# Expert layers of a two-block kernel: the second table as the streamed operand of its products

## The chip, the core and the metric

The kernel runs on one core of a Trainium2 chip. The metric is the device time of one execution in microseconds (us). Engines are named as the profile names them: PE is TensorE (matrix products; PEld is its loading of the stationary operand, the weights), DVE is VectorE, ACT is ScalarE, POOL is GpSimd, and SP is SyncE, whose queue issues the DMAs here.

## What is computed

The reference is a chain of two blocks of two layers each, over 256 tokens of 1024 features, all in fp32. The change lies in the two expert layers (`peer_ffn`, one in each layer of the first block). Each has 16384 experts; an expert is a row of a first table `u_tab` and a row of a second table `v_tab`:

```python
def block(args):
    hx, idx, g = args                      # 128 tokens, their chosen experts, gates
    u = u_tab[idx]
    act = jax.nn.gelu(jnp.einsum('thkd,td->thk', u, hx).astype(jnp.float32))
    return jnp.einsum('thk,thkd->td', g * act, v_tab[idx])
...
mod = (cond @ w_ada[i] + b_ada[i])[:, None, :]
sh1, sc1, g1, sh2, sc2, g2 = jnp.split(mod, 6, axis=-1)
...
x = x + g2 * peer_ffn(h, peer_w_q[i], peer_keys[i], peer_u[i], peer_v[i])
```

The second thing of interest is the modulation, `mod`: a product of one vector with a table of 1024 by 6144 for each layer. The part of it for layer 1 that is left is computed during the expert layer of layer 0.

## The kernel before, in words

**Data.** Activations lie features by tokens: a tile has 128 features on its partitions and 256 tokens along its columns. Every product is made of three products of a rounded format (fp32r): each operand is split into a high part and the rest, and high x high, high x rest and rest x high are added up in PSUM. `mm3` (lines 414 to 419) issues the three: L416 weight high and activation high, L417 weight high and activation rest, L418 weight rest and activation high. In the trace they read `psmm<-xh,whi`, `psmm<-xl,whi` and `psmm<-xh,wlo`: the output, then the streamed operand, then the stationary one.

**Weights.** A `Stream` (lines 255 to 296) reads a table in blocks of 128 partitions by 1024 columns (512 KB). A block lands in one of four `raw` buffers; ACT casts it to `whi` (L283), DVE subtracts to get `wlo` (L285); there are three buffers of each. SP's queue is strictly in order: a DMA that waits for its buffer holds all DMAs behind it.

**The expert layer** (`peer`, from line 1151). It does not gather rows. It multiplies the tokens with all of the first table (128 chunks of 128 experts), applies gelu and the gates (zero for experts that a token didn't choose), and keeps the result in `A`, 128 experts by 128 chunks by 256 tokens. The change is in what follows, the sum over the second table. For each chunk `c` of 128 experts (`chunk`, L1253) one block of V is read and split; every second chunk also splits two chunks of `A` into `xh` (ACT, L464) and `xl` (DVE, L465), which are called `wh` and `wl` in the code. `product` (L1259) then makes, for each of the eight groups `o` of 128 features, the three products with a 128x128 piece of V as the stationary operand and 256 tokens as the streamed one: 24 products of 256 columns for a chunk. The sums, features by tokens, collect in four PSUM banks over all 128 chunks. I call this stretch the V stage, V0 in layer 0 and V1 in layer 1.

**The modulation in V0.** `ada_sums` (L704) reads 48 blocks of 512 KB through the same `raw` buffers; for each DVE issues one product-and-add with a running row (L712 and L714, written to `oh`), and after every eight PE adds the row up over partitions (L718). In the code a step is issued after every second chunk from chunk 9 on.

**The end of the stage.** The last three chunks are held back (`last`) and run feature group by feature group. While a pair of groups is in work, the evacuation of the pair before runs: `residual` (L743) adds the sum to the residual (L753, DVE), makes the next projection's leading operand (`lead.tile`: L314 on ACT, L315 on DVE) and squares for the norm (L487, ACT). `lead.products` are 96 products of the next layer's first projection that need no norm; the rest of that projection waits for the norm (L503, L504, L551, L552).

**Order.** A scheduler sets the order on each engine's queue from the code's dependences and its own costs; engines then run their queues in order.

Of the kernel before, what the change touches and what calls it, by code (L numbers as in the profile page):

```python
# [114 lines left out]
WO = 1, 2  # L115
SQB = 2
NST = 4
PL = 1, 3
ADDED, ADDED_LN = 6, 4

# [134 lines left out]
class Stream:  # L255
# [1 line left out]

    def __init__(s, ker, name, lo_pool=None, hi_dve=None, store=()):  # L260
        s.ker, s.name, s.ap = ker, name, ker.d[name]
        s.lo_pool, s.hi_dve, s.store = lo_pool, hi_dve, store
        s.b = 0
        s.tiles = []

    def prefetch(s, pin=False):

        k, b = s.ker, s.b
        if b == s.ap.shape[0]:
            return  # L270
        s.b += 1
        nc = k.nc
        keep = k.pin if pin else lambda ins: ins
        raw = k.raw_block(s.ap[b])
        if b < len(s.store):
            hi, lo = s.store[b]
        else:
            hi = k.splp.tile([128, WBLK], F32R, name="whi", tag="whi")
            lo = k.splp.tile([128, WBLK], F32R, name="wlo", tag="wlo")
        if s.hi_dve and s.hi_dve(b):  # L280
            keep(nc.vector.tensor_copy(hi, raw))
        else:
            keep(nc.scalar.copy(hi, raw))  # L283
        eng = nc.gpsimd if s.lo_pool and s.lo_pool(b) else nc.vector
        keep(eng.tensor_tensor(lo, raw, hi.bitcast(F32), op=OP.subtract))  # L285
        s.tiles += [(hi[:, j * 128:(j + 1) * 128], lo[:, j * 128:(j + 1) * 128]) for j in range(8)]

    def __iter__(s):
        return s
# [53 lines left out]
class Ker:  # L343
# [357 lines left out]
                                                   op0=OP.add, op1=OP.subtract)  # L701
        return hi, lo

    def ada_sums(s, layer, r, acc):  # L704
# [446 lines left out]
    def peer(s, layer, x):  # L1151
# [3 lines left out]
        with s.tc.tile_pool(name="peer", bufs=1) as P:  # L1155
# [91 lines left out]
                        applied = S  # L1247

            wh, wl = s.acts()
            acc = [s.mm().rearrange("p (a b) -> p a b", a=2) for _ in range(4)]  # L1250
            vt = s.stream(f"V{layer}")

            def chunk(c):  # L1253
                if c % 2 == 0:
                    sl = slice(c % 8, c % 8 + 2)
                    s.split_into(wh[:, sl, :], wl[:, sl, :], A[:, c:c + 2, :])
                return [next(vt) for _ in range(KD)], (wh[:, c % 8, :], wl[:, c % 8, :])

            def product(c, o, v, w):  # L1259
                s.mm3(acc[o // 2][:, o % 2, :], v[o], w, c == 0 and o % 2 == 0, c == NK - 1, skip_group_check=True)  # L1260

            extra = iter(())
            if layer == 0:
                extra = chain(*(s.ada_sums(1, r, oh.rearrange("p a b c d -> p (a b c d)").bitcast(F32)[:, 0:WBLK])
                                for r in range(3)))
            NL = 3
            for c in range(NK - NL):
                v, w = chunk(c)
                for o in range(KD):
                    product(c, o, v, w)  # L1270
# [15 lines left out]
            for j in range(KD // 2):  # L1286
                for o in (2 * j, 2 * j + 1):
                    for c, v, w in last:
                        product(c, o, v, w)
                for f in after:  # L1290
                    f()
                after = [ev(o, acc[j][:, o % 2, :]) for o in (2 * j, 2 * j + 1)]
            for f in after:
                f()
            lead.products()
# [529 lines left out]
```

## Time and profile before

| | |
|---|---|
| median of three timed runs | 3094.58 us (3094.17 to 3098.24) |
| the profiled execution | 3085.98 us |
| its span, first to last instruction | 3084.2 us |
| PE busy | 2924.4 us, 95% |
| DVE busy | 2242.0 us, 73% |
| ACT busy | 1489.4 us, 48% |
| POOL busy | 434.6 us, 14% |
| V0, first to last product of V | 785.2 to 1171.0 us |
| V1, last product of V | 2196.0 us |

PE's busy time is of modelled ends: a product of 256 columns is listed with some 0.28 us, while the next one starts about 0.12 us after it. What a product takes of the stage is therefore read from the distance of two starts, not from its listed length. The same holds, less strongly, for DVE: its instructions overlap by a few hundredths of a us.

### The profile page before, as it was taken

How to read it: one execution, taken by the hardware profiler on the slowest of the kernel's cores; microseconds unless marked ns; L12 is line 12 of the kernel's file. 1: busy time of each engine (PE TensorE's matmuls, PEld its weight loads, DVE VectorE, ACT ScalarE, POOL GpSimd, SP SyncE). 2: the span in 40 equal slices, each digit the busy share in tenths (PEclk: the TensorE clock that was granted, in tenths of full speed). 3: DMA queues.
4: the chain of work that ended last, by engine and by line, in shares of the span. 5: the costliest groups of instructions: out<-in, count | busy, mean ns of one | idle time of the engine just before them, and what ended most of it. 6: DMA issues, size and time to landing. Idle time of an engine off the chain costs nothing. (4 is left out here: it accounts for less than half of the span.)

```text
span 3084.2 us, 58197 instructions
## 1 busy us (share of the span) xinstructions
PE 2924.4 (95%) x23408; PEld 2824.4 (92%) x23408; DVE 2242.0 (73%) x4113; ACT 1489.4 (48%) x2576; POOL 434.6 (14%) x260
## 2 busy tenths in 40 slices
PE   7999989999999998698999999999999989998898
PEld 7988989999999997698999999999988889977898
DVE  7897996777567658899777765555663588665885
ACT  3335534444444445554444444444654666555663
POOL 2232330000000003523300000000123020111201
PEclk9999999999999998899999999999999999998999
DMA  6664445444677863354544456655435246543464
GB/s 251 205 189 155 154 140 165 144 145 151 198 260 259 263 218 122 115 168 156 159 143 144 146 159 183 184 184 182 156 100 75 89 145 184 181 123 81 143 185 131
DMA packets 139999, 503.66 MB, mean 163 GB/s; under 512 B 15800, under 2 KB 18504, under 8 KB 139344
## 3 DMA queue, kind: packets, MB, share of 16 engines
q1 hardware_dynamic: 139728, 499.93, 52.8%
q8 instruction: 184, 3.01, 0.4%
q14 instruction: 87, 0.71, 0.1%
HBM read 496.72 MB, written 1.05 MB: 161 GB/s over the span
## 5 line engine op out<-in xcount | busy, mean ns | idle before, releaser
L416 PE MATMUL psmm<-xh,whi 128*128 128x256 f32 x5488 | 1568.4, 288 | 43.2 <-ACT xh L464 18.3
L418 PE MATMUL psmm<-xh,wlo 128*128 128x256 f32 x5488 | 1558.8, 286 | 33.3 <-DVE wlo L285 20.9
L417 PE MATMUL psmm<-xl,whi 128*128 128x256 f32 x5488 | 1564.0, 286 | 3.9 <-DVE xl L465 1.9
L283 ACT CAST whi<-raw 128x1024 fp32r<-128x1024 f32 x819 | 857.5, 1048 | 1094.3 <-PE psmm L417 781.4
L285 DVE TENSOR_TENSOR wlo<-raw,whi 128x1024 fp32r<-128x1024 f32 x740 | 936.6, 1268 | 446.1 <-ACT whi L283 434.0
L416 PEld LDWEIGHTS psmm<-xh,whi 128*128 128x128 f32 x5488 | 1059.9, 194 | 56.0 <-ACT xh L464 19.9
L418 PEld LDWEIGHTS psmm<-xh,wlo 128*128 128x128 f32 x5488 | 1060.3, 194 | 37.9 <-DVE wlo L285 24.1
L417 PEld LDWEIGHTS psmm<-xl,whi 128*128 128x128 f32 x5488 | 1063.1, 194 | 8.1 <-DVE xl L555 3.3
L285 POOL TENSOR_TENSOR wlo<-raw,whi 128x1024 fp32r<-128x1024 f32 x90 | 249.6, 2778 | 460.9 <-ACT whi L283 416.4
L285 POOL TENSOR_TENSOR Ar<-raw,Ar 128x1024 fp32r<-128x1024 f32 x4 | 9.6, 2408 | 1361.1 <-ACT Ar L283 1361.1
L1190 DVE TENSOR_TENSOR oh<-io,sel 128x512 f16<-128x512 f16 x128 | 54.4, 425 | 105.2 <-PE psac L1202 52.7
L416 PE MATMUL psst<-xh,whi 128*128 128x256 f32 x400 | 119.9, 301 | 0.0
L417 PE MATMUL psst<-xl,whi 128*128 128x256 f32 x400 | 118.4, 297 | 0.3 <-DVE xl L646 0.3
L418 PE MATMUL psst<-xh,wlo 128*128 128x256 f32 x400 | 117.9, 295 | 0.7 <-DVE wlo L285 0.7
L1202 PEld LDWEIGHTS <-oh 128*128 128x128 f16 x1024 | 103.8, 118 | 6.9
L416 PE MATMUL psmm<-yh,whi 128*128 128x256 f32 x352 | 98.0, 279 | 0.0
L418 PE MATMUL psmm<-yh,wlo 128*128 128x256 f32 x352 | 97.6, 278 | 0.0
L417 PE MATMUL psmm<-yl,whi 128*128 128x256 f32 x352 | 97.2, 276 | 0.0
L714 DVE SCALAR_TENSOR_TENSOR oh<-raw,cond,oh 128x1024 f32<-128x1024 f32 x42 | 53.9, 1284 | 56.8 <-DMA raw<-in_ada 56.6
L465 DVE TENSOR_TENSOR xl<-A,xh 128x512 fp32r<-128x512 f32 x128 | 87.1, 684 | 0.0
L417 PEld LDWEIGHTS psst<-xl,whi 128*128 128x128 f32 x400 | 79.0, 197 | 7.3 <-issue 5.6
L418 PEld LDWEIGHTS psst<-xh,wlo 128*128 128x128 f32 x400 | 79.0, 198 | 5.0 <-issue 3.5
(574 smaller groups left out, 4031.8 us busy)
## 6 DMA issues: line engine op xcount, KB each, us to landing
raw<-in_U SPq DMA_DIRECT2D x256, 512.0 KB, 3.6
raw<-in_V SPq DMA_DIRECT2D x256, 512.0 KB, 4.2
raw<-in_up SPq DMA_DIRECT2D x88, 512.0 KB, 4.0
raw<-in_ada SPq DMA_DIRECT2D x80, 512.0 KB, 4.4
raw<-in_down SPq DMA_DIRECT2D x44, 512.0 KB, 3.7
raw<-in_ev_in SPq DMA_DIRECT2D x42, 512.0 KB, 3.6
raw<-in_hg_in SPq DMA_DIRECT2D x40, 512.0 KB, 3.9
raw<-in_peer_q SPq DMA_DIRECT2D x32, 512.0 KB, 3.6
```

What stands on the lines that cost most here:

```text
L283: keep(nc.scalar.copy(hi, raw))
L285: keep(eng.tensor_tensor(lo, raw, hi.bitcast(F32), op=OP.subtract))
L416: first = t.matmul(ps, w[0], x[0], start=start, stop=False, **kw)
L417: t.matmul(ps, w[0], x[1], start=False, stop=False, **kw)
L418: t.matmul(ps, w[1], x[0], start=False, stop=stop, **kw)
L465: s.nc.vector.tensor_tensor(lo, src, hi.bitcast(F32), op=OP.subtract)
L714: nc.vector.scalar_tensor_tensor(acc, raw, s.cond[:, k:k + 1], acc, op0=OP.mult, op1=OP.add)
L1190: nc.vector.tensor_tensor(o1, io4, k1, op=OP.is_equal)
L1202: ins = nc.tensor.matmul(pv[:, t, :], oh[:, g % 2, 0, :, t], oh[:, g % 2, 1 + e, :, t], start=e == 0, stop=e == 1)
```

## The change

Three things change.

1. The roles of the operands in the V stage are swapped. `Stream` gets a width, so that V's block is handed on whole. The stationary operand is now a piece of the activations (128 experts by 128 tokens, two token tiles `tt`), the streamed one is half of V's block (512 features, two halves). A chunk has 2 x 2 x 3 = 12 products of 512 columns. Four PSUM banks hold one sum each, of 128 tokens by 512 features.
2. The sums now lie tokens by features. At the end of the stage they are copied to SBUF (`tok`, two copies by ACT and two by DVE, in two `raw` buffers) and transposed back on PE, sixteen transposes of 128x128 in four PSUM tiles; `residual` reads those.
3. The modulation's blocks in V0 no longer share the `raw` buffers. They land in four pieces of `A` that hold the first sixteen chunks, which are used up by then. A step is issued after every second chunk from chunk 17 on.

```diff
-        s.tiles += [(hi[:, j * 128:(j + 1) * 128], lo[:, j * 128:(j + 1) * 128]) for j in range(8)]
+        s.tiles += [(hi[:, j:j + s.width], lo[:, j:j + s.width]) for j in range(0, WBLK, s.width)]
...
-                raw = s.raw_block(s.d[f"ada{layer}"][((r - 1 + layer) * KD + k) * 2 + e])
+                ap = s.d[f"ada{layer}"][((r - 1 + layer) * KD + k) * 2 + e]
+                if room:
+                    raw = room[k % len(room)]
+                    nc.sync.dma_start(raw, ap)
+                else:
+                    raw = s.raw_block(ap)
...
-            acc = [s.mm().rearrange("p (a b) -> p a b", a=2) for _ in range(4)]
-            vt = s.stream(f"V{layer}")
+            acc = [[s.mm() for _ in range(2)] for _ in range(2)]
+            vt = s.stream(f"V{layer}", width=WBLK)
...
-            def product(c, o, v, w):
-                s.mm3(acc[o // 2][:, o % 2, :], v[o], w, c == 0 and o % 2 == 0, c == NK - 1, skip_group_check=True)
+            def product(c, half, tt, v, w):
+                ts, fs = slice(tt * 128, (tt + 1) * 128), slice(half * 512, (half + 1) * 512)
+                for i, (a, b) in enumerate(((0, 0), (0, 1), (1, 0))):
+                    nc.tensor.matmul(acc[half][tt], w[a][:, ts], v[b][:, fs], start=c == 0 and i == 0,
+                                     stop=c == NK - 1 and i == 2)
...
+                room = [Af[:, n * WBLK:(n + 1) * WBLK] for n in range(RAW_A)]
...
-                if c % 2 and c > 8:
+                if c % 2 and c >= 4 * RAW_A:
                     next(extra, None)
...
+            def features(half, tok):
+                for j in range(2):
+                    pt = s.ac().rearrange("p (a b) -> p a b", a=2)
+                    for e in range(2):
+                        for tt in range(2):
+                            nc.tensor.transpose(pt[:, e, tt * 128:(tt + 1) * 128],
+                                                tok[:, tt, (2 * j + e) * 128:(2 * j + e + 1) * 128], s.ident)
+                    yield [ev(4 * half + 2 * j + e, pt[:, e, :]) for e in range(2)]
...
+                    (nc.vector.tensor_copy if tt else nc.scalar.copy)(tok[:, tt, :], acc[half][tt])
```

The scheduler's order changes with it. Three places matter for the prediction.

**PE in the V stage.** Before, two feature groups of one chunk (`psmm_9022` is a bank, `xh` and `xl` the activations' parts, `whi` and `wlo` V's):

```order
L418 MATMUL psmm_9022<-xh_9017,wlo_13085 128x256
L416 MATMUL psmm_9022<-xh_9017,whi_13092 128x256
L417 MATMUL psmm_9022<-xl_9018,whi_13092 128x256
L418 MATMUL psmm_9022<-xh_9017,wlo_13093 128x256
L416 MATMUL psmm_9022<-xh_9017,whi_13098 128x256
```

Now, one whole chunk:

```order
L1271 MATMUL psmm_9019<-whi_11544,xh_9017 128x512
L1271 MATMUL psmm_9020<-whi_11544,xh_9017 128x512
L1271 MATMUL psmm_9021<-whi_11544,xh_9017 128x512
L1271 MATMUL psmm_9022<-whi_11544,xh_9017 128x512
L1271 MATMUL psmm_9019<-wlo_11545,xh_9017 128x512
L1271 MATMUL psmm_9019<-whi_11544,xl_9018 128x512
L1271 MATMUL psmm_9020<-wlo_11545,xh_9017 128x512
L1271 MATMUL psmm_9020<-whi_11544,xl_9018 128x512
L1271 MATMUL psmm_9021<-wlo_11545,xh_9017 128x512
L1271 MATMUL psmm_9021<-whi_11544,xl_9018 128x512
L1271 MATMUL psmm_9022<-wlo_11545,xh_9017 128x512
L1271 MATMUL psmm_9022<-whi_11544,xl_9018 128x512
```

Half as many products of twice the width; the four that need only the high part come first, in four banks.

**DVE and SP in V0.** Before, on DVE (`oh` is the modulation's running row, `raw_9399` and `raw_9464` its blocks):

```order
L285 TENSOR_TENSOR wlo_9306<-raw_9303,whi_9305 128x1024
L714 SCALAR_TENSOR_TENSOR oh_3390<-raw_9399,cond_90,oh_3390 128x1024
L285 TENSOR_TENSOR wlo_9342<-raw_9339,whi_9341 128x1024
L465 TENSOR_TENSOR xl_9018<-A_2917,xh_9017 128x512
L285 TENSOR_TENSOR wlo_9372<-raw_9369,whi_9371 128x1024
L714 SCALAR_TENSOR_TENSOR oh_3390<-raw_9464,cond_90,oh_3390 128x1024
```

Now, on DVE:

```order
L286 TENSOR_TENSOR wlo_9350<-raw_9347,whi_9349 128x1024
L719 TENSOR_SCALAR oh_3390<-A_2917,cond_90 128x1024
L721 SCALAR_TENSOR_TENSOR oh_3390<-A_2917,cond_90,oh_3390 128x1024
L466 TENSOR_TENSOR xl_9018<-A_2917,xh_9017 128x512
L721 SCALAR_TENSOR_TENSOR oh_3390<-A_2917,cond_90,oh_3390 128x1024
L286 TENSOR_TENSOR wlo_9373<-raw_9370,whi_9372 128x1024
L721 SCALAR_TENSOR_TENSOR oh_3390<-A_2917,cond_90,oh_3390 128x1024
L286 TENSOR_TENSOR wlo_9391<-raw_9388,whi_9390 128x1024
```

and on SP's queue in the same stretch, before and now:

```order
L395 DMA raw_9464<-in_ada1 128x1024
L395 DMA raw_9469<-in_V0 128x1024
L395 DMA raw_9499<-in_V0 128x1024
L395 DMA raw_9529<-in_ada1 128x1024
L395 DMA raw_9534<-in_V0 128x1024
```

```order
L396 DMA raw_9468<-in_V0 128x1024
L715 DMA A_2917<-in_ada1 128x1024
L396 DMA raw_9490<-in_V0 128x1024
L715 DMA A_2917<-in_ada1 128x1024
L396 DMA raw_9508<-in_V0 128x1024
L715 DMA A_2917<-in_ada1 128x1024
```

The 48 modulation steps stood one to two chunks from chunk 7 to chunk 106; they now stand about one to a chunk, on DVE from chunk 3 to chunk 54 of V0.

**PE at the end of V0.** Before, the last product of V is followed by those of the next layer (`Ar` holds the leading operand and its weights):

```order
L417 MATMUL psmm_9022<-xl_9018,whi_13098 128x256
L418 MATMUL psmm_9022<-xh_9017,wlo_13099 128x256
L416 MATMUL psac_13247<-Ar_13103 128x258
L416 MATMUL psac_13248<-Ar_13103 128x258
L416 MATMUL psmm_13249<-Ar_13103 128x258
```

Now the transposes (`cst` holds the identity) stand between:

```order
L1271 MATMUL psmm_9022<-whi_11550,xl_9018 128x512
L1307 MATMUL psac_11622<-cst_80,tok_11580 128x128
L1307 MATMUL psac_11637<-cst_80,tok_11580 128x128
L1307 MATMUL psac_11622<-cst_80,tok_11580 128x128 x3
L1307 MATMUL psac_11637<-cst_80,tok_11580 128x128 x3
L1307 MATMUL psac_11654<-cst_80,tok_11601 128x128 x4
L417 MATMUL psmm_11691<-Ar_11555 128x258
```

All twelve products of the last chunk run before the first transpose, and the first addition to the residual comes behind both of DVE's copies.

## Rows read from the trace of the kernel before

**Rows 1.** The page: busy time by engine; PE's clock in 40 slices.

```profile
PE 2924.4 (95%) x23408; PEld 2824.4 (92%) x23408; DVE 2242.0 (73%) x4113; ACT 1489.4 (48%) x2576; POOL 434.6 (14%) x260
...
PEclk9999999999999998899999999999999999998999
```

**Rows 2.** Groups by form, V1 from 1850 to 2150: count | busy, mean ns | idle.

```profile
L418 PE MATMUL psmm<-xh,wlo 128*128 128x256 f32 x834 | 236.0, 283 | 0.0
L416 PE MATMUL psmm<-xh,whi 128*128 128x256 f32 x834 | 236.0, 283 | 0.0
L417 PE MATMUL psmm<-xl,whi 128*128 128x256 f32 x834 | 236.0, 283 | 0.0
...
L285 DVE TENSOR_TENSOR wlo<-raw,whi 128x1024 fp32r<-128x1024 f32 x105 | 128.6, 1225 | 142.5 <-ACT whi L283 142.5
L283 ACT CAST whi<-raw 128x1024 fp32r<-128x1024 f32 x105 | 109.9, 1047 | 165.4 <-PE psmm L417 165.4
```

**Rows 3.** Busy time in stretches: start, V0, its end, half clock, V1.

```profile
core 0: us, PE busy (x) PEld busy (x) DVE busy (x) ACT busy (x) POOL busy (x), PEclk, DMA share, GB/s
10.00:30.00 20.00, 17.70 (x127) 15.60 (x125) 18.73 (x26) 4.93 (x9) 5.14 (x2) 1.00 1.03 409
768.00:870.00 102.00, 94.37 (x768) 91.97 (x767) 59.36 (x65) 43.72 (x56) 0.00 (x0) 1.00 0.62 204
870.00:1120.00 250.00, 250.00 (x2057) 245.12 (x2056) 173.79 (x170) 111.46 (x130) 0.00 (x0) 1.00 0.80 262
...
1186.00:1191.00 5.00, 4.41 (x18) 3.40 (x17) 4.82 (x12) 2.68 (x6) 0.00 (x0) 0.64 0.00 0
...
1191.90:1193.20 1.30, 1.30 (x8) 1.30 (x8) 1.30 (x6) 0.58 (x1) 0.00 (x0) 0.50 0.06 13
...
1810.00:2175.00 365.00, 362.52 (x3007) 362.12 (x3006) 193.33 (x194) 165.87 (x195) 0.00 (x0) 1.00 0.59 181
```

**Rows 4.** Waits from 768 to 870: total us, times, longest.

```profile
DVE oh L714 <- DMA raw<-in_ada: 20.1, 7, 4.1
...
PE psmm L418 <- DVE wlo L285: 5.2, 5, 1.5
```

**Rows 5.** PE in order of time where it runs at half clock: start, length.

```profile
1192.09 0.41 PE L416 MATMUL psac<-xh,whi 128*128 128x256 f32 x1
1192.30 0.41 PE L417 MATMUL psac<-xl,whi 128*128 128x256 f32 x1
1192.51 0.41 PE L418 MATMUL psac<-xh,wlo 128*128 128x256 f32 x1
```

**Rows 6.** PE in order of time, same form with another streamed operand (`yh`, `yl`).

```profile
2655.73 0.28 PE L416 MATMUL psmm<-yh,whi 128*128 128x256 f32 x1
...
2656.52 0.28 PE L417 MATMUL psmm<-yl,whi 128*128 128x256 f32 x1
```

**Rows 7.** DVE in order of time in V0: start, length, idle before.

```profile
846.80 1.28 DVE L714 SCALAR_TENSOR_TENSOR oh<-raw,cond,oh 128x1024 f32<-128x1024 f32 x1 [2.70 <-DMA raw<-in_ada]
848.00 1.22 DVE L285 TENSOR_TENSOR wlo<-raw,whi 128x1024 fp32r<-128x1024 f32 x1
849.13 0.69 DVE L465 TENSOR_TENSOR xl<-A,xh 128x512 fp32r<-128x512 f32 x1
849.74 1.22 DVE L285 TENSOR_TENSOR wlo<-raw,whi 128x1024 fp32r<-128x1024 f32 x1
```

**Rows 8.** Modulation's work on PE in V0; transposes with the product after them.

```profile
1116.31 1.05 PE L718 MATMUL psst<-oh,cst 128*32 128x512 f32 x4
...
920.38 0.60 PE L729 MATMUL psac<-cst,adarow 128*128 128x128 f32 x4
920.73 0.36 PE L417 MATMUL psmm<-xl,whi 128*128 128x256 f32 x1
```

**Rows 9.** End of V0: DVE's first residual sum, PE's products around it.

```profile
1167.60 0.88 DVE L753 SCALAR_TENSOR_TENSOR xres<-psmm,io,xres 128x256 f32<-128x256 f32 x2 [0.41 <-PE psmm L418]
...
1170.99 0.41 PE L416 MATMUL psac<-Ar 128*128 128x258 f32 x2
...
1185.26 0.38 PE L416 MATMUL psmm<-xh,whi 128*128 128x256 f32 x1 [1.20 <-ACT xh L552]
```

**Rows 10.** Groups by form elsewhere: DVE reading 512 columns of PSUM.

```profile
L1457 DVE TENSOR_TENSOR RAW<-RAW,psmm 128x512 f32<-128x512 f32 x18 | 12.3, 685 | 14.0 <-PE psmm L1456 14.0
```

More of the change, by code (lines that the diff above doesn't have):

```diff
@@ L117 @@
 NST = 4
+RAW_A = 4
 PL = 1, 3
@@ L255, with __init__ @@
 class Stream:
-    def __init__(s, ker, name, lo_pool=None, hi_dve=None, store=()):
+    def __init__(s, ker, name, lo_pool=None, hi_dve=None, store=(), width=128):
         s.ker, s.name, s.ap = ker, name, ker.d[name]
         s.lo_pool, s.hi_dve, s.store = lo_pool, hi_dve, store
-        s.b = 0
+        s.b, s.width = 0, width
         s.tiles = []
@@ L702, in first_norm, with ada_sums @@
         return hi, lo
-    def ada_sums(s, layer, r, acc):
+    def ada_sums(s, layer, r, acc, room=()):
         nc = s.nc
@@ L1256, in chunk @@
                     s.split_into(wh[:, sl, :], wl[:, sl, :], A[:, c:c + 2, :])
-                return [next(vt) for _ in range(KD)], (wh[:, c % 8, :], wl[:, c % 8, :])
-            def product(c, o, v, w):
-                s.mm3(acc[o // 2][:, o % 2, :], v[o], w, c == 0 and o % 2 == 0, c == NK - 1, skip_group_check=True)
+                return next(vt), (wh[:, c % 8, :], wl[:, c % 8, :])
+            def product(c, half, tt, v, w):
[3 more added lines that the diff above has]
+                                     stop=c == NK - 1 and i == 2)
             extra = iter(())
             if layer == 0:
-                extra = chain(*(s.ada_sums(1, r, oh.rearrange("p a b c d -> p (a b c d)").bitcast(F32)[:, 0:WBLK])
-                                for r in range(3)))
+                room = [Af[:, n * WBLK:(n + 1) * WBLK] for n in range(RAW_A)]
+                row = oh.rearrange("p a b c d -> p (a b c d)").bitcast(F32)[:, 0:WBLK]
+                extra = chain(*(s.ada_sums(1, r, row, room) for r in range(3)))
             NL = 3
@@ L1268, in peer @@
                 v, w = chunk(c)
-                for o in range(KD):
-                    product(c, o, v, w)
-                if c % 2 and c > 8:
+                for half in range(2):
+                    for tt in range(2):
+                        product(c, half, tt, v, w)
+                if c % 2 and c >= 4 * RAW_A:
                     next(extra, None)
@@ L1284, in peer @@
             ev = s.residual(layer, 1, lead, gs)
-            after = []
[L1286 to L1292, printed above, removed]
+            def features(half, tok):
+                for j in range(2):
+                    pt = s.ac().rearrange("p (a b) -> p a b", a=2)
+                    for e in range(2):
+                        for tt in range(2):
+                            nc.tensor.transpose(pt[:, e, tt * 128:(tt + 1) * 128],
+                                                tok[:, tt, (2 * j + e) * 128:(2 * j + e + 1) * 128], s.ident)
+                    yield [ev(4 * half + 2 * j + e, pt[:, e, :]) for e in range(2)]
+            toks = []
+            for half in range(2):
+                tok = s.rawp.tile([128, WBLK], F32, name="tok", tag="raw").rearrange("p (a b) -> p a b", a=2)
+                for tt in range(2):
+                    for c, v, w in last:
+                        product(c, half, tt, v, w)
+                    (nc.vector.tensor_copy if tt else nc.scalar.copy)(tok[:, tt, :], acc[half][tt])
+                toks.append(tok)
+            after = []
+            for half, tok in enumerate(toks):
+                for fs in features(half, tok):
+                    for f in after:
+                        f()
+                    after = fs
             for f in after:
```

## The prediction

> **What bounds the kernel now.** I read the page first: PE is busy for 95% of the span, the next engine, DVE, for 73%, and PE's clock is at its upper level, 2.4 GHz, nearly throughout [rows 1]. So PE looks like the bound, but its busy time is of modelled ends, and the share is a mean. I therefore read the stages that change. In V1 from 1850 to 2150 us PE starts 3 x 834 = 2502 products in 300 us, one each 0.1199 us, without idle, while DVE and ACT wait: ACT for buffers that PE sets free, DVE for ACT [rows 2]. V1 is bound by the distance of PE's products and by nothing else. V0 is so only from 870 us on; before that PE is busy for 94.4 of 102 us [rows 3], and the waits say why: DVE stands before a modulation step that waits for its block (20.1 us in 7 waits), the split of V is queued behind it, and PE waits 5.2 us in five stalls for `wlo` [rows 4].
>
> The question is then what sets 0.1199 us. 256 columns at 2.4 GHz are 0.1067 us, so 0.0132 us is something else. Where the clock is at its lower level, 1.2 GHz (granted 0.50 of full [rows 3]), the same form advances by 0.21 us [rows 5], which is 256 / 1.2 = 0.213 and leaves nothing over. So the extra doesn't grow with the clock's period and is not added to every product: it hides once a product streams for 0.213 us. The likely cause is the hand-over to the next weights, for which 0.107 us of streaming is too short a cover. Its size is not fixed by the shape either: with `yh` and `yl` streamed, the form takes (2656.52 - 2655.73) / 7 = 0.113 us, over seven steps of which the first and the last row stand there [rows 6].
>
> **The change part by part.**
>
> *Wide products.* A chunk has 24 products before, 24 x 0.1199 = 2.878 us, and 12 of 512 columns after. No row shows this form. Its lower bound is streaming alone, 512 / 2.4 = 0.2133 us, the time that the rows at half clock show with the cover of 0.213 us. Its upper bound with the mechanism above is 0.2133 + 0.0132 = 0.2265, if the extra stays once per product. I take 0.216, a fifth of the way, since the rows at half clock show no extra at the same length. That gives 12 x 0.216 = 2.592 us and saves 0.286 us a chunk, over 2 x 128 chunks 73.2 us; the bounds give 81.5 and 40.7 us. All of it lies on the path as long as the feeders keep up: in V1 DVE needs 1.13 + 0.61 / 2 = 1.44 us a chunk by the distances of its starts [rows 7], ACT 1.05 us and half of a cast of `A`, and DMA, which moves 181 GB/s at 2.88 us a chunk [rows 3], would move 202. None comes near.
>
> The Trainium skill, in "TensorE: Matmul & The Clock Gate", section "Back-to-back issue gap", gives N / 2.4 + 2.5 ns for products in a row. As an estimate by that page 256 columns would take 0.109 and 512 columns 0.216 us, and the change would save only (24 x 0.1092 - 12 x 0.2158) x 256 = 8 us. The trace agrees with no 0.109: it shows 0.1199 in V1.
>
> *The modulation in V0.* The 48 steps and their blocks are the same, their places are not. What goes are the five stalls, 5.2 us. What comes is density: 48 steps to 51 chunks instead of to 100. Count the stretch from the first to the last modulation DMA, which holds 48 blocks of V too. DVE: 48 x (1.13 + 0.61 / 2 + 1.20) = 126.5 us [rows 7]. PE: 48 x 2.592 + 6 x 1.05 + 3 x 0.35 for the modulation's own products and transposes [rows 8] = 131.8 us. DMA: 96 blocks of 0.524 MB are 50.3 MB, 123 us at the 409 GB/s that the queue reached at the kernel's start, 153.5 us at the 328 GB/s that V0's 262 GB/s at a share of 0.80 make [rows 3]. So DVE fits with 5 us to spare, and the queue may or may not. Bounds: 0 and 153.5 - 131.8 = 21.7 us. I take 8: the order places most of the modulation's DMAs four chunks of buffers ahead of the step that needs them, where before it was two or three, but bursts of three or four steps stand on DVE in a row, and behind them PE waits for `wlo`. The four products that need only `whi` come first and give it 0.86 us of cover.
>
> *The end of each stage.* Before, DVE's first residual sum starts at 1167.60, 3.39 us ahead of the end of V's products at 1170.99; from there a chain over eight features (DVE, ACT and POOL), the norm and the next split leads to the first product that needs it, at 1185.26 [rows 9]. PE's lead products fill some 11.5 us of that. After, no sum can start before all products are done and DVE has made both of its copies out of PSUM: about 0.2 us for the last product and 0.69 for a copy [rows 10]. So the chain starts 3.39 + 0.9 = 4.3 us later against the end of V; up to 1 us comes back, since the sums no longer come at the pace of pairs. The transposes, four in 0.35 us [rows 8], are sixteen in 1.4 us and lie beside the chain but for the first ones. I take 4 us for each layer, 8 in all, with bounds of 2 and 9 each; the upper one is the lead products at half clock, 96 x (0.213 - 0.12) = 8.9 us. The scheduler's small moves in the stages that follow I cost at nothing.
>
> *Sum.* -73.2 - 5.2 + 8 + 8 = -62.4 us. The profiled execution took 3085.98 us and would take 3023.6; it lies 8.6 us under the median of the timed runs. Against that median, 3094.58, I predict 3032 us.
>
> **The rivals.**
>
> *The hand-over stays once per product* (0.2265 us). For: 0.113 with `yh` shows that where the operands lie matters, and the operands now change places. Against: the rows at half clock. -40.7 - 5.2 + 8 + 8 = -30, 3065 us.
>
> *V0's dense stretch is bound by the queue* at 328 GB/s, +21.7 instead of +8: 3046 us. For: no stretch of V0 moved more than that. Against: V0 asked for no more.
>
> *The clock falls at the ends.* The row from 1186 to 1191 has 0.64 of full clock, after PE had thinned out [rows 3]; the transposes thin it out sooner. With 9 us for each end instead of 4 it is 3042 us. The Trainium skill says in the same page, section "Part 4: PE-mode transpose", that transposes take about 275 ns in a kernel and do not count as PE being busy. As an estimate by the page 32 of them are 8.8 us. The trace shows four in 0.35 us at full clock, between other products.
>
> *Width gives nothing:* the 0.0132 us is a share of each column's streaming at full clock (reading the operand, say), and 512 columns take 0.2398. Then the sum is 0 - 5.2 + 8 + 8 = +11 us, 3105. It decides from 0.2363 us a product on. Against it: 0.113 us with another operand, and nothing over at half clock, though that would also fit a reading limit. The page's gap formula stands near this rival, as it sees little to gain.
>
> *The slower side:* the queue in V0. If the dense stretch gets only the 204 GB/s of V0's first part [rows 3], 50.3 MB take 246.6 us, 114.8 more than PE needs, and the sum is +44, 3139 us. It decides where the stretch takes 131.8 + 70.4 = 202 us, which is 249 GB/s. Against it: the 204 was what was asked for, at a share of 0.62.
>
> *Better than forecast:* 0.2133 us, no stall in V0 and 2 us for each end give -82.7, 3012 us.
>
> **How the numbers follow.** The forecast has 0.60; the hand-over 0.13, the dense stretch 0.10, the clock 0.07, no gain by width 0.04, the slower side 0.03, the better case 0.03. The likeliest is 3032. From 3012 to 3068 the range holds all but the two bad cases, some of the better one and the mixtures that lie beyond. A measurement tells about 0.2%, 6 us, from no change. Faster is every case but the two bad ones, 0.93; half of the case without gain may fall within 0.2%, so same has 0.02 and slower 0.05.
>
> **What would show it.** In V1 the starts of the 512-column products stand 0.216 us apart, with no idle; 0.2265 is the first rival, 0.24 the fourth. V1's products of V last some 332 us instead of 368. In V0 PE's idle time lies within the first 55 chunks and is under 22 us; the DMA share there is above 0.9, and the rate near 380 GB/s. After chunk 60 V0 looks like V1. From the last product of V to the first product behind the norm it is 18 us instead of 14.3, at full clock. The prediction is wrong if the wide products are not at 0.213 to 0.227 us, or if PE waits in V0 for more than these 22 us.

## The result and the profile after

The changed kernel takes 3046.43 us, the median of four runs (3043.19 to 3050.42), beside 3095.32 us for the kernel before on the same chip. The ratio is 0.9841, with a 95% interval of 0.9824 to 0.9858: 1.6% faster, 49 us. The forecast was 3032, with a range of 3012 to 3068. The profiled execution is the one of 3050.42 us, with a span of 3048.6 us. It is the slowest of its four, while the profiled execution of before is faster than any timed run of before; the two profiles are therefore only 35.6 us apart.

The page of after, busy time and PE's clock, to be set beside [rows 1]:

```profile
PE 2887.5 (95%) x20368; PEld 2666.7 (87%) x20368; DVE 2260.8 (74%) x4117; ACT 1491.1 (49%) x2580; POOL 422.2 (14%) x260
...
PEclk9999999999999998899999999999999999998999
```

PE has 3040 recorded instructions fewer and is the bound as before; the clock's pattern is the same.

Groups by form in V1 from 1850 to 2150 us, after: count | busy, mean ns | idle. They answer to [rows 2].

```profile
L1271 PE MATMUL psmm<-wlo,xh 128*128 128x512 f32 x442 | 172.1, 389 | 0.0
L1271 PE MATMUL psmm<-whi,xl 128*128 128x512 f32 x441 | 171.9, 390 | 0.0
...
L1271 PE MATMUL psmm<-whi,xh 128*128 128x512 f32 x442 | 118.3, 390 | 0.0
L284 ACT CAST whi<-raw 128x1024 fp32r<-128x1024 f32 x110 | 115.6, 1051 | 77.5 <-PE psmm L1271 77.5
```

1325 products in 300 us are one each 0.2264 us. A chunk takes 12 x 0.2264 = 2.717 us in place of 2.878, 0.161 us less, and 256 chunks give 41 us. PE is never idle, and ACT still waits for PE. So the stage is bound by the distance of PE's products as before; that distance is not the 0.216 us of the forecast, but its upper bound.

Busy time in stretches of after, as in [rows 3]. They are V0's first part, the middle of its dense part (the modulation's steps run on DVE from 794 to 944 us), V0 from 870 us on, its end, and V1:

```profile
core 0: us, PE busy (x) PEld busy (x) DVE busy (x) ACT busy (x) POOL busy (x), PEclk, DMA share, GB/s
787.50:870.00 82.50, 82.11 (x360) 65.88 (x361) 69.78 (x73) 39.22 (x47) 0.00 (x0) 1.00 0.92 335
830.00:920.00 90.00, 90.00 (x397) 71.00 (x397) 81.99 (x82) 41.39 (x49) 0.00 (x0) 1.00 0.99 372
870.00:1145.50 275.50, 275.50 (x1214) 223.97 (x1212) 183.29 (x178) 131.00 (x150) 2.52 (x2) 1.00 0.69 232
1146.00:1167.00 21.00, 16.76 (x119) 16.10 (x119) 15.56 (x28) 11.81 (x26) 6.29 (x6) 0.92 0.52 172
1808.00:2156.00 348.00, 347.69 (x1534) 288.02 (x1535) 201.87 (x194) 168.70 (x193) 2.40 (x1) 1.00 0.60 191
```

Up to 870 us the queue moves 335 GB/s at a share of 0.92, against 204 at 0.62 before, and PE is idle for 0.4 us of 82.5. In the middle of the dense part the DMA engines are busy nearly all the time (372 GB/s at a share of 0.99), DVE is busy for 82 of 90 us, and PE is still never idle. Waits of V0, 787 to 1146 us of after, beside [rows 4]:

```profile
DVE oh L721 <- DMA A<-in_ada: 5.2, 2, 2.6
...
DVE oh L719 <- DMA A<-in_ada: 1.4, 1, 1.4
...
PE psmm L1271 <- DVE wlo L286: 0.2, 1, 0.2
```

DVE's wait for the modulation's blocks has fallen from 20.1 us in 7 waits (in a quarter of the stage) to 6.6 us in three in the whole stage (L719 is the first step of each running row, L721 the others), and PE's wait for `wlo` from 5.2 to 0.2 us.

The end of V0 in order of time, after (start, length, engine, operation, idle before), which answers to [rows 9]:

```profile
1144.25 1.05 ACT L284 CAST Ar<-raw 128x1024 fp32r<-128x1024 f32 x1 [1.37 <-DMA raw<-in_lru_xb]
...
1145.27 0.39 PE L1271 MATMUL psmm<-whi,xl 128*128 128x512 f32 x1
1145.32 1.28 ACT L510 ACT_TABLE_LOAD   x1
...
1145.75 0.69 DVE L1317 COPY tok<-psmm 128x512 f32<-128x512 f32 x1 [0.27 <-PE psmm L1271]
...
1146.72 1.05 ACT L1317 COPY tok<-psmm 128x512 f32<-128x512 f32 x2
...
1147.34 1.09 PE L1307 MATMUL psac<-cst,tok 128*128 128x128 f32 x8 [1.69 <-ACT tok L1317]
...
1148.14 1.27 DVE L760 SCALAR_TENSOR_TENSOR xres<-psac,io,xres 128x256 f32<-128x256 f32 x3 [1.71 <-PE psac L1307]
...
1166.71 0.39 PE L417 MATMUL psmm<-xh,whi 128*128 128x256 f32 x1 [2.16 <-ACT xh L553]
```

From the start of V's last product to the first product behind the norm it is 1166.71 - 1145.27 = 21.4 us; before it was 14.3 from the product behind the last one [rows 9], and so 14.4 by this count. DVE's copies come when I had them. ACT, however, first casts a block of the next layer's weights (`Ar`), which had to wait for its DMA, then loads a table, and copies its two quarters behind that; PE's transposes wait for ACT. At V1's end it is 19.6 us.

### The profile page after: what moved, and what is told of

The parts are those of the page before. It is cut to its first block, busy times and chain, and to the rows that moved or that the text cites. A ratio compares the mean times of both kernels' runs of the same rounds, so it can differ in the third digit from the quotient of the medians.

```text
span 3048.6 us, 52246 instructions
## 1 busy us (share of the span) xinstructions
PE 2887.5 (95%) x20368; PEld 2666.7 (87%) x20368; DVE 2260.8 (74%) x4117; ACT 1491.1 (49%) x2580; POOL 422.2 (14%) x260
## 3 DMA queue, kind: packets, MB, share of 16 engines
HBM read 496.72 MB, written 1.05 MB: 163 GB/s over the span
## 5 line engine op out<-in xcount | busy, mean ns | idle before, releaser
L417 PE MATMUL psmm<-xh,whi 128*128 128x256 f32 x3440 | 989.6, 291 | 43.2 <-ACT xh L465 14.1
L419 PE MATMUL psmm<-xh,wlo 128*128 128x256 f32 x3440 | 981.3, 288 | 33.3 <-DVE wlo L286 21.3
L418 PE MATMUL psmm<-xl,whi 128*128 128x256 f32 x3440 | 985.6, 288 | 2.7 <-DVE xl L556 1.6
L417 PEld LDWEIGHTS psmm<-xh,whi 128*128 128x128 f32 x3440 | 667.2, 195 | 50.7 <-ACT xh L465 15.3
L419 PEld LDWEIGHTS psmm<-xh,wlo 128*128 128x128 f32 x3440 | 668.6, 195 | 37.6 <-DVE wlo L286 24.5
L418 PEld LDWEIGHTS psmm<-xl,whi 128*128 128x128 f32 x3440 | 670.2, 195 | 6.7 <-DVE xl L556 3.6
L1271 PE MATMUL psmm<-wlo,xh 128*128 128x512 f32 x1024 | 399.8, 390 | 0.2 <-DVE wlo L286 0.2
L1271 PE MATMUL psmm<-whi,xl 128*128 128x512 f32 x1024 | 397.9, 390 | 0.0
L1271 PE MATMUL psmm<-whi,xh 128*128 128x512 f32 x1024 | 277.6, 390 | 3.6 <-ACT xh L465 3.6
L1271 PEld LDWEIGHTS psmm<-whi,xl 128*128 128x128 f32 x1024 | 192.4, 188 | 39.5
```

Of the source, the lines that this page charges most:

```text
L417: first = t.matmul(ps, w[0], x[0], start=start, stop=False, **kw)
L418: t.matmul(ps, w[0], x[1], start=False, stop=False, **kw)
L419: t.matmul(ps, w[1], x[0], start=False, stop=stop, **kw)
L1271: nc.tensor.matmul(acc[half][tt], w[a][:, ts], v[b][:, fs], start=c == 0 and i == 0, stop=c == NK - 1 and i == 2)
```

## The experiments

Two questions were open: what sets the 0.0133 us that a product takes beyond its streaming, and what the second part and the ends are worth by themselves. In what follows "the changed kernel" is the one after the change.

**Width or roles.** The table still streams and the tokens are the weights, but each product is cut in two:

```diff
-                ts, fs = slice(tt * 128, (tt + 1) * 128), slice(half * 512, (half + 1) * 512)
+                ts = slice(tt * 128, (tt + 1) * 128)
+                for q in range(2):
+                    fs = slice(half * 512 + q * 256, half * 512 + (q + 1) * 256)
```

> The changed kernel, with the table still streamed past the tokens' weights, but each product of 512 columns cut into two of 256, so 24 in a chunk as before. If the width is what saved time: 0.120 us from start to start again, 2.88 us a chunk, V0 and V1 each about 39 / 2 = 20 us longer, some 3085 us in all. If it is the exchange of roles (table streamed, tokens as weights) that saved it: 0.1135 us from start to start, no change against the changed kernel's 3046 us.

Measured: 3089.85 us in one run. Busy time in a stretch of its V1 (length, PE busy and count, granted clock, DMA share, rate):

```profile
1870.00:2140.00 270.00, 270.00 (x2252) 1.00 0.60 183
```

270 / 2252 = 0.120 us. So the width saves the time, and the exchange of roles by itself saves nothing: 24 products pay the extra 24 times, 12 pay it 12 times. This also refutes the rival by which the extra is a share of each column's streaming: 512 columns would take 0.2398 us in one product as in two halves.

**Where the operands lie.** All operands lie in SBUF at places that the program fixes. By the sizes of the tiles in the code, the split activations `xh` begin a multiple of 256 bytes behind the table's `whi` in both kernels (what lies between takes 4096 or 1024 bytes a tile). `yh`, which streams faster [rows 6], does not: a tile of 704 bytes lies ahead of it, 192 more than a multiple of 256. Five kernels move them with unused bytes, which change no instruction. The first has 64 bytes between the table's buffers and the activations:

```diff
         s.actp = ctx.enter_context(tc.tile_pool(name="act", bufs=1))
+        s.actp.tile([128, 16], F32, name="pad", tag="pad")
```

> The changed kernel with one unused tile of 64 bytes a partition placed ahead of the split activations `xh` and `xl` (and of everything behind them in that pool), so that these lie 64 bytes further on against the split table `whi` and `wlo`; nothing else differs. Theory A (each product pays a fixed extra of 0.0133 us for its change of weights, wherever its operands lie): 512-column products of V stay 0.227 us apart, 256-column products with `xh` streamed stay at 0.120, the time stays within 5 us of 3046 us. Theory B (the extra depends on where the streamed operand lies against the weights, as the 0.113 us with `yh` streamed hints): the 256-column products go to 0.113 us, those of 512 columns to 0.220; with 3072 wide ones and some 12,000 narrow ones that is 15,000 x 0.0067 = 100 us less, about 2946 us.

The others have 32 and 192 bytes at this place, or 64 and 32 bytes at the head of the first pool, where table and activations move together:

```diff
         s.cpool = ctx.enter_context(tc.tile_pool(name="cst", bufs=1))
+        s.cpool.tile([128, 16], F32, name="pad", tag="pad")
```

> The changed kernel with the unused 64 bytes ahead of everything that matters, table and activations, so that distances between them are as in the changed kernel and all of them lie 64 bytes further on. Relative theory (the distance of the streamed operand from the weights sets the extra): 0.120 us for products with `xh`, 0.113 with `yh`, 0.227 for those of 512 columns, as in the changed kernel. Absolute theory (each operand's own place sets it): `xh` and `yh` lie where they lie with the first pad, so 0.118 and 0.120 us; what the wide ones do is open, since the streamed table now moves too.

> As the run before it in this table of runs, with 32 bytes in place of 64: all operands lie 32 bytes further on, which takes them from odd multiples of 32 bytes to multiples of 64. Relative theory: nothing changes (0.120, 0.113, 0.227 us). Absolute theory with a cost for a start off a 64-byte line: all of these fall, to 0.113 us or below for 256 columns and 0.220 or below for 512.

> The changed kernel with 32 unused bytes between the table's buffers and the activations, so that these lie 32 bytes further on and the table stays. Relative theory: a distance that none of the other runs has, so the 256-column products with `xh` leave 0.120 and 0.118 us, to either side. Absolute theory: `xh` and `yh` as in the run with all shifted by 32 bytes. Theory A of the first run (a fixed extra for each product) is already at odds with 0.118 and 0.231 to 0.236 us there.

> The changed kernel with 192 unused bytes between the table's buffers and the activations. Over the runs so far a product's distance to the next goes with (address of the streamed operand - address of the weights) modulo 256 bytes: 0 gives 0.120 us, 64 gives 0.118, 192 gives 0.113 (`yh`) for 256 columns; 0 gives 0.227, 192 and 224 give 0.233 for 512. Here `xh` and `xl` come to 192 and the wide products to 64. If the rule holds: 0.113 to 0.114 us for the products with `xh`, as with `yh`; the wide ones open. If the 0.113 is a property of `yh` and not of its place: 0.117 or 0.120.

Measured in two stretches in which PE is never idle: V1 with wide products, and the last layer's projection with narrow ones. The columns are again length, PE busy and count, clock, share, rate. First the changed kernel:

```profile
1850.00:2120.00 270.00, 270.00 (x1193) 1.00 0.61 193
2510.00:2570.00 60.00, 60.00 (x503) 1.00 0.58 181
```

All moved by 32 bytes (by 64 the counts are 1193 and 502):

```profile
1850.00:2120.00 270.00, 270.00 (x1193) 1.00 0.59 193
2510.00:2570.00 60.00, 60.00 (x503) 1.00 0.58 183
```

64 bytes between table and activations:

```profile
1850.00:2120.00 270.00, 270.00 (x1159) 1.00 0.59 187
2510.00:2570.00 60.00, 60.00 (x512) 1.00 0.60 186
```

32 bytes between them:

```profile
1850.00:2120.00 270.00, 270.00 (x1159) 1.00 0.58 188
2510.00:2570.00 60.00, 60.00 (x517) 1.00 0.56 187
```

192 bytes between them:

```profile
1850.00:2120.00 270.00, 270.00 (x1182) 1.00 0.60 191
2510.00:2570.00 60.00, 60.00 (x512) 1.00 0.60 189
```

The counts hold one or two products that only reach into the stretch; taken off, they give these distances, in us:

| kernel | time of the kernel | wide | narrow |
|---|---|---|---|
| changed kernel | 3046.43 (median of 4) | 0.2265 | 0.120 |
| all moved, 32 bytes | 3048.60 (one run) | 0.2265 | 0.120 |
| all moved, 64 bytes | 3045.22 (one run) | 0.2265 | 0.120 |
| between, 32 bytes | 3045.30 (one run) | 0.233 | 0.1165 |
| between, 64 bytes | 3052.98 (median of 4) | 0.233 | 0.118 |
| between, 192 bytes | 3028.78 (one run) | 0.2285 | 0.118 |

The fixed extra (theory A) falls: unused bytes alone move the wide products from 0.2265 to 0.233 us. The absolute theory falls: moving everything together changes no distance by more than the rows can tell. What counts is how things lie to each other, the activations (with what lies behind them) against the table. This also tells `yh` apart, which the same 64 bytes bring to a multiple of 256 bytes behind `whi`. Its stretch in the changed kernel, then with the 64 bytes between:

```profile
2610.00:2620.00 10.00, 10.00 (x90) 1.00 0.61 193
```

```profile
2610.00:2620.00 10.00, 10.00 (x86) 1.00 0.61 200
```

0.113 us becomes 0.119: `yh` loses what it had, and with that the 0.113 was a matter of place, not of `yh`. Theory B had the direction for narrow products and not the size: 64 bytes give 0.118, not 0.113. For wide ones it had the wrong direction: they cost 1536 x 2 x 0.0065 = 20 us, and V0 and V1 are 9 and 10 us longer in the profile. The rest of the kernel gives most of that back, so that it is only 6.5 us slower than the changed one (ratio to the kernel before 0.9862, 0.9846 to 0.9879, an interval that overlaps with that of the changed kernel). At 0.233 us the wide products also lie above 0.2265, which the prediction had as their upper bound.

**Each kind of product at its own distance.** One tile holds both halves of the activations; it begins 192 bytes further on, and in the V stages they lie 64 bytes further still, which makes 256:

```diff
+        s.actp.tile([128, 48], F32, name="pad", tag="pad")
...
-    def acts(s, kt=KD):
-        hi = s.actp.tile([128, kt, S], F32R, name="xh", tag="xh")
-        lo = s.actp.tile([128, kt, S], F32R, name="xl", tag="xl")
-        return hi, lo
+    def acts(s, kt=KD, off=0):
+        x = s.actp.tile([128, 2 * kt * S + 16], F32R, name="xh", tag="xh")
+        return [x[:, off + n * kt * S:off + (n + 1) * kt * S].rearrange("p (k s) -> p k s", k=kt) for n in range(2)]
...
-            wh, wl = s.acts()
+            wh, wl = s.acts(off=16)
```

> The changed kernel with each stage's activations at the distance that suits it: the two halves `xh` and `xl` lie in one tile that begins 192 bytes further on, and in the V stages 64 bytes further still, so that the narrow products have the distance 192 modulo 256 and the wide ones 0, as in the changed kernel. By the rule: 0.227 us for wide ones, 0.113 to 0.114 for the narrow ones, of which there are some 12,000: 12,000 x 0.006 = 72 us less where PE alone sets the pace; the U stages' feeders may hold part of it back, so 2975 to 3010 us. If the rule doesn't hold for `xh`: 3040 to 3050 us.

Measured: a ratio of 0.9776 to the kernel before (0.9754 to 0.9798), with runs of 3017.89, 3020.76 and 3030.04 us; a fourth, of 5489.93 us, is not counted. The same stretches:

```profile
1850.00:2120.00 270.00, 270.00 (x1193) 1.00 0.61 193
2510.00:2570.00 60.00, 60.00 (x531) 1.00 0.60 194
```

The wide products are back at 0.2265 us, the narrow ones at 60 / 529 = 0.1134. But not everywhere: from 560 to 680 us, in the first stage of the expert layer, this kernel has 1019 instructions where the changed one has 1006 and the one with 64 bytes 1019, so there the narrow products stay at 0.118:

```profile
560.00:680.00 120.00, 120.00 (x1019) 1.00 0.47 147
```

That is a part of why some 25 us came in place of 72. In this stretch the feeders have nothing to do with it, since PE isn't idle. It also shows that the rule "distance of streamed operand and weights, modulo 256" is not the whole of it: from 2510 to 2570 this kernel and the one with 192 bytes have the same distances between `xh`, `xl` and the table, and yet 0.1134 and 0.118 us. They differ in what lies behind (`yh` among it, 192 here and 128 there, which ACT and DVE write in that stretch). Which accesses meet there isn't settled.

**The second part undone.** The modulation's blocks go through the shared buffers again:

```diff
-                room = [Af[:, n * WBLK:(n + 1) * WBLK] for n in range(RAW_A)]
+                room = ()
...
-                if c % 2 and c >= 4 * RAW_A:
+                if c % 2 and c > 8:
```

> The changed kernel with the second part undone: the modulation's blocks go through the shared buffers `raw` again, one step behind every odd chunk from 9 on. By my reading of the trace after, the dense stretch costs V0 only 1 to 2 us of PE's waiting, and spread out as before it would cost about 5: V0 3 to 4 us longer, 3050 us, within the noise of 0.2%. A rival says that the second part carries much of the gain (the shared buffers held V back by more than PE's stalls show, since V now runs faster and asks the queue for more): 10 us or more, 3056 us and above.

Measured: 3066.80 us, ratio to the kernel before 0.9905 (0.9888 to 0.9921), so 20 us are lost. Its waits in V0, 788 to 1166 us:

```profile
DVE oh L721 <- DMA raw<-in_ada: 82.8, 42, 3.7
...
PE psmm L1271 <- DVE wlo L286: 12.3, 10, 2.2
...
DVE oh L719 <- DMA raw<-in_ada: 10.9, 6, 4.1
```

DVE stands before each of its 48 modulation steps for the block, and PE behind it ten times. V0's products take 376.5 us in place of 357.6. Of these 19 us 12 are PE's waits; the granted clock is also down to 0.97 in two stretches of 50 us (890 to 940 and 990 to 1040). My 3 to 4 us are refuted, the rival holds. The likely reason is that a chunk that is 0.16 us shorter leaves the shared buffers less time: the five stalls of the kernel before become ten longer waits.

**The second part alone**, in the kernel before:

```diff
+                room = [Af[:, n * WBLK:(n + 1) * WBLK] for n in range(4)]
...
-                if c % 2 and c > 8:
+                if c % 2 and c >= 16:
```

> The kernel before, with only the second part of the change: the modulation's blocks go into rows of `A`, at every odd chunk from the sixteenth on; V keeps its 24 products of 256 columns. If the rows of `A` are worth in the old kernel what its trace shows (five stalls of 5.2 us in V0) and the 20 us that undoing them costs the changed kernel come from the shorter chunk (2.72 in place of 2.88 us): 5 us less, 3090 us, hardly to be told from no change. If the rows are worth the same whatever the products' width: 3075 us.

Measured: 3091.90 us, ratio 0.9987 (0.9977 to 0.9996), 4 us less. Its waits from 768 to 870 us show one PE wait of 2.3 us for `wlo`, where five stood that took 5.2 us together [rows 4]:

```profile
DVE oh L717 <- DMA A<-in_ada: 3.3, 1, 3.3
...
PE psmm L418 <- DVE wlo L285: 2.3, 1, 2.3
```

So the parts are not additive. The second alone is worth 4 us, the first alone 29 (3095 to 3067), both together 49: 16 us belong to the pair.

**The end in another order.** The last three chunks' products are held in the order of the code, and the residual's setup (and with it the table load) comes behind ACT's copies:

```diff
-            ev = s.residual(layer, 1, lead, gs)
...
-                        product(c, half, tt, v, w)
+                        product(c, half, tt, v, w, s.pin)
...
                 toks.append(tok)
+            ev = s.residual(layer, 1, lead, gs)
```

> The changed kernel with the end of each V stage put in another order: the last three chunks' products are held in the order in which the code has them (a half of the features at a time, so that the first halves' sums are copied out while PE goes on), and the residual's setup, with its load of a table into ACT, comes behind ACT's copies out of PSUM instead of ahead of them. If the ends cost what they do because the copies and the chain behind them begin only after the last product and behind the table load: the first residual sum starts before the last product ends, and from the last product to the first one behind the norm it is 14 to 17 us in place of 21.2 and 19.4, some 8 to 10 us less in all, 3037 us. If the chain of eight features and the norm sets it, wherever it starts: 19 us or more still, and at most 3 us less.

Measured: 3066.70 us, ratio 0.9907 (0.989 to 0.9923), 20 us slower than the changed kernel. From the last product to the one behind the norm it is 19.1 us in both layers, not 14 to 17, so the second reading holds; the scheduler still put the transposes of both halves behind the last product. Busy time around the two ends of V:

```profile
core 0: us, PE busy (x) PEld busy (x) DVE busy (x) ACT busy (x) POOL busy (x), PEclk, DMA share, GB/s
1138.00:1148.00 10.00, 6.63 (x21) 4.53 (x20) 6.04 (x4) 5.75 (x7) 4.22 (x2) 0.83 0.54 173
2153.00:2165.00 12.00, 9.05 (x26) 6.39 (x25) 6.48 (x5) 5.24 (x6) 4.73 (x2) 0.72 0.55 167
```

PE waits for `wlo` (once for 2.1 us), and its granted clock falls in the stretch. The likely reason is that half a chunk of each of three chunks in a row asks for splits twice as fast as they come. V0 and V1 get 5 and 6 us longer. Some 11 us more are lost in stages that the edit doesn't touch in the code, most of them behind V1; why, I didn't trace.

**The table load alone** is moved in the next kernel; the order of the products is left.

> The changed kernel with the residual's setup, and so ACT's load of a table, behind ACT's two copies of sums instead of ahead of them; the order of the last products is left to the scheduler. If the load delays the first copies: the first residual sum comes 1.3 us sooner after V's last product (1.4 in place of 2.7 us) in V0, and the first product behind the norm 1 to 1.5 us sooner. If DVE's copies or PE's transposes set it: less than 0.5 us.

Measured: 3043.66 us in one run. Its end of V0, in order of time:

```profile
1144.35 0.40 PE L1271 MATMUL psmm<-whi,xl 128*128 128x512 f32 x1
...
1144.58 1.04 PE L1305 MATMUL psac<-cst,tok 128*128 128x128 f32 x8
...
1144.98 1.28 ACT L510 ACT_TABLE_LOAD   x1
1145.45 1.65 DVE L760 SCALAR_TENSOR_TENSOR xres<-psac,io,xres 128x256 f32<-128x256 f32 x4
...
1162.83 0.38 PE L417 MATMUL psmm<-xh,whi 128*128 128x256 f32 x1 [2.16 <-ACT xh L553]
```

The first residual sum stands 1145.45 - 1144.35 = 1.1 us behind the last product's start, not 2.9, and the product behind the norm 18.5, not 21.4; in V1 it is 18.3 in place of 19.6. So in the profile of the changed kernel the load stood on the path. But these 3 and 1.3 us aren't what it costs each time. The five kernels with moved operands, the one with both distances and the one with the second part undone have the changed kernel's instructions at these ends, and their 14 ends take 18.2 to 19.8 us. The kernel with 64 bytes between comes to 18.5 and 18.2 us with the load where it was. Its end of V0:

```profile
1145.84 1.05 ACT L284 CAST Ar<-raw 128x1024 fp32r<-128x1024 f32 x1 [1.02 <-DMA raw<-in_lru_xb]
...
1146.91 1.28 ACT L511 ACT_TABLE_LOAD   x1
...
1148.53 0.40 PE L1272 MATMUL psmm<-whi,xl 128*128 128x512 f32 x1
...
1149.74 0.88 DVE L761 SCALAR_TENSOR_TENSOR xres<-psac,io,xres 128x256 f32<-128x256 f32 x2
...
1167.02 0.38 PE L418 MATMUL psmm<-xh,whi 128*128 128x256 f32 x1 [2.16 <-ACT xh L554]
```

Here the cast of `Ar` starts 2.7 us before V's last product and not 1.0 as in the changed kernel's profile, so that the load is done before that product, and the first residual sum stands 1.2 us behind its start. What the load costs thus depends on when the block for the cast ahead of it lands: from nearly nothing to some 3 us. One run doesn't show a gain in the kernel's time.

**Both together**, the two distances and the later load:

> The placement of the run with both distances and the later table load of the last run, together. The places give what they gave (narrow products 0.113 to 0.118 us, wide ones 0.227), the table load some 1.3 to 3 us at each V stage's end: 3 to 5 us below the 3021 us of the undisturbed runs with both distances, so 3016 us. If the two don't add up (the copies' order is left to the scheduler, and other moves may come with it): 3018 us or more.

Measured: 3014.96 us, the median of five runs (3010.91 to 3029.63), ratio 0.9757 (0.9733 to 0.9781): 2.4% faster than the kernel before, and the fastest kernel of this study. The ends are as in the last run (18.5 and 18.3 us), the distances as in the kernel with both. Whether it beats that one can't be told, as the intervals overlap.

## Why the prediction was right, and where its sum was not

**The side and the range** were right: 3046 lies between the forecast and the first rival, within 3012 to 3068. The forecast of 3032 was 14 us too fast, and the agreement is better than the terms deserve: the largest of them was 32 us too big, and half of that was made up by gains that the sum didn't have.

**The wide products** are the term that was mis-sized. The sum took 73.2 us; V1 shows 0.2264 us, which is the first rival's 0.2265 and the lower bound of the gain, 41 us. The step that failed is "I take 0.216, a fifth of the way, since the rows at half clock show no extra at the same length". It supposed that the extra hides beneath 0.213 us of streaming. At full clock the wide products stream for just as long and pay the 0.013 us, so cover isn't what the half clock gave. The change that halves the number of products halves the number of extras, and no more. Why no extra shows at half clock stays open. The reason that I gave the extra, the hand-over of weights, is not shown by any run either: unused bytes alone move it between 0.007 and 0.013 us for narrow products and between 0.013 and 0.020 for wide ones. The remark on the first rival, that `yh` shows that the place matters, was the right lead, and I didn't follow it to a rule.

**The Trainium skill's rule** in "TensorE: Matmul & The Clock Gate", section "Back-to-back issue gap", would, as an estimate, have put the wide products at 0.216 us. The section itself calls N / 2.4 + 2.5 ns the gap of an isolated product and states about 131 ns for 512 columns in a stream, which I left out. The runs show 0.2265 to 0.233 us, so the measurement decides against both figures for this form. The formula is 0.0107 us low for either form, and so misses 12 x 0.0107 x 256 = 33 us of the saving that V1's rows show.

**The modulation.** I had -5.2 us for the old stalls and +8 for the dense stretch. The stalls are gone, and the dense stretch costs PE 0.4 us of idle time by the rows above. V0's products take 357.6 us and V1's 348.1; of the 9.5 us between them some 7.4 are the modulation's own products by the prediction's count (6 x 1.05 + 3 x 0.35), so that 2 us at most are the price of the dense stretch. The bursts of modulation steps on DVE that I feared do not reach PE. The rival of a queue at 328 GB/s is refuted: from 830 to 920 us it moved 372. Its share of 0.99 there says that it was near its limit for a while, as I had thought possible, but PE got what it needed. What I missed has no place in the sum and yet decided: with shorter chunks the old arrangement costs 20 us, as the kernel with the second part undone shows, and that kernel's 12 us of PE's waits are most of it. The two parts of the change need each other.

**The ends** cost 7.0 us in V0 and 5.1 in V1 (19.6 against 14.5), 12 in all where I had 8, within the bounds of 2 and 9 each. The 14 ends with the same code in other kernels, 18.2 to 19.8 us, cost some 4 to 5 each, so that 8 was about right, and V0's 7.0 lies above them all. I timed DVE's copies and the transposes; ACT's two copies and the cast and the table load ahead of them were not among my steps, and PE's transposes wait for these. The chain itself kept its length: from the first residual sum to the product behind the norm it is 17.7 us before [rows 9] and 1166.71 - 1148.14 = 18.6 after. The rival of a falling clock explains little: 0.92 over V0's end.

**What is not accounted for.** With the measured terms the sum is -41 - 5 + 1.5 + 12 = -32 us, or 3062, where 3046 was measured. The two profiles are 36 us apart. In them V0 and V1 take 28.1 and 24.1 us less, 52 in all where the terms give 44.5. V1's 24.1 are some 20 from the products; the rest lies mostly in the old V1's first 6 us, where PE waited and its granted clock was 0.73, and which I had at nothing. The ends take 12 us more. Against the gain, the first stages of the expert layers are 10.5 us longer in the profile of after, although the change leaves their instructions as they are: 138.9 and 157.1 us between the same two reciprocals on DVE, against 133.9 and 151.6 (in layer 0 from that of `hrstd` to the gates' first, in layer 1 from the norm's to the gates' second). It isn't the change: the kernel with the second part alone, which has the old V stages, shows 138.9 and 155.5 us, and so does every other profile in which the activations lie as before against the table (138.8 to 139.6 and 155.5 to 158.5). So the profiled execution of before was most likely a lucky one there. It lies 9.3 us under the median of before, and that of after 4.0 above its own, which makes the 13 us by which the medians are further apart than the profiles. Some 6 us of the profiles' 36 are spread over other stages and aren't explained.

## What to carry to other kernels

A stage that is bound by the distance of its products can pay an extra for each product; twice the width halved the number of extras here and not their size, so a form that no row shows is best taken at its upper bound, and even that holds only for the place where it was measured. When two rows of one form differ (0.113 and 0.120 us here), move the operands by some unused bytes: it is a cheap experiment, and here it was worth half as much as the change. When a stage gets faster, ask again of each shared buffer whether its old slack still covers the traffic that goes through it.

## What the runs showed of the hardware that was not expected

- The distance of two products depends on how operands lie to each other in SBUF; the operands' own distance modulo 256 bytes doesn't settle it alone (0.1134 and 0.118 us at the same one). With everything moved together by 32 or 64 bytes nothing changes (0.120 and 0.2265 us); with 32 to 192 bytes between table and activations narrow products take 0.113 to 0.118 us and wide ones 0.2285 to 0.233. Narrow and wide products want different places: of those tried, a multiple of 256 bytes is the slowest for the narrow ones and the fastest for the wide ones.
- At half clock no extra shows (0.21 us for 256 columns [rows 5]), at full clock with the same streaming time it does (0.2265 for 512).
- ACT's table load takes 1.28 us and stands in its queue where the program puts the setup: here ahead of two copies that PE waited for, at a price between nearly nothing and 3 us for each end, by when the block for the cast ahead of it landed.
- The same instructions of a stage took 134 us in one profile and 139 in eight others of kernels that agree there. Differences of that size between single profiles say nothing on a change.
- With the DMA engines at a share of 0.99 (372 GB/s) and DVE busy for 82 of 90 us, PE was still never idle over these 90 us.
